# Hybrid diffusion step on one core: a pair's seven products add up in three places of the accumulator

## The chip, the cores and the metric

One Trainium2 chip, one of its cores. The kernel is one launch; what is measured is its device time in microseconds. TensorE multiplies matrices into PSUM, the accumulator. VectorE and ScalarE read PSUM and work on SBUF, GpSimd does a few fills, and SyncE issues the transfers from and to the main memory.

## The reference

Two layers with the same form run over 512 latent tokens and 128 context tokens, 640 in all, of 1024 features each. Per layer:

```python
shift1, scale1, gate1, shift2, scale2, gate2 = split(silu(cond) @ w_ada + b_ada)
h = rms_norm(x) * (1 + scale1) + shift1
q, k, v, og, gkf, gkb, sb, sc, sx, fx, mg = split(h @ w_in)
# A: bidirectional chunked gated linear attention, 4 heads; B: sb * conv3(sc * sx); C: Re(2-D DFT(fx))
x = x + gate1 * ((sigmoid(mg_A) * (A @ w_a_out) + sigmoid(mg_B) * (B @ w_b_out) + sigmoid(mg_C) * (C @ w_c_out)) @ w_o)
h = rms_norm(x) * (1 + scale2) + shift2
x = x + gate2 * ((silu(h @ w_gate) * (h @ w_up)) @ w_down)
```

A final RMSNorm follows, and the last attention states of the context tokens are returned as well. Everything is in fp32.

## The kernel before, in words

Features lie on the 128 partitions and tokens along the columns, in two halves of 320 (`TH`). A product in fp32 accuracy is three passes of TensorE: weights and activations are each split into a rounded high part (a cast, on ScalarE for the weights, L140) and the remainder (a subtraction on VectorE, L141), and high x high, high x low and low x high are added (`mm3`). A matmul has 128 x 128 weights and 320 columns.

Most products with 1024 features in are done for two blocks of 128 output columns at once, by `pair` (L245), with the seven products of Strassen and Winograd in place of eight. Each of the seven runs over four blocks of features and three passes, so it is 12 matmuls, and a pair is 84. There are 24 pairs in the mixer of each layer (names w1p_n: v, branch gates, convolution and Fourier inputs) and 19 in each feed-forward stage (wup_n), 86 in all.

The weights of a pair come in two loads and are taken in four chunks. Chunk a is [A11 A12] as loaded and serves two products, b and c are sums of the quarters (L162 to L168) and serve two each, d is A22 and serves one. The right-hand sides are the features h (B11, B21, B22 in the code) and the sums T1 to T4 of the token halves, which `token_sums` makes once per stage.

The names of the products, in the order of before: B11 with a, B21 with a, T2 with b, T3 with b, T1 with c, B22 with c, T4 with d. Their results go into four PSUM tiles pa, pb, pc, pd of two halves each (0:320 and 512:832). ScalarE copies the first (L265), and VectorE forms the two results by four additions (L269, L271, L275, L279) into an SBUF tile z.

PSUM is a pool of four such tiles of 1024 fp32 columns (L101), shared by pairs, the dense blocks (`dense`), the modulation products (`ada`) and the attention heads. Between two pairs of a mixer, after two of every three pairs, stand the matmuls of a quarter of a modulation vector, whose weights come as two raw chunks that need no split. Attention heads and the Fourier mixing are generators that a pair advances by `tick_bg`, twice.

All loads of weights are issued by SyncE in one stream with six buffers; a new load is issued when buffers are counted as freed (by the split of chunk d, by that of a full chunk, or when a raw chunk is taken). `prefetch` (L186) splits weights ahead of their use: at each `take` it goes on until two chunks are in front of the ones taken, of which d chunks are not counted. Split weights have three buffers for high and three for low parts, and one small one for d.

The order of instructions on each engine isn't the program's. A planner puts it together when the kernel is built, from the program's order as priority, the dependences between tiles and its own estimate of times; an instruction that is not ready by that estimate is passed by later ones of the same engine. The order is fixed from then on, and semaphores hold an instruction until what it needs is done.

Of the kernel before, what the change touches and what calls it, by code (L numbers as in the profile page):

```python
# [19 lines left out]
P = 128  # L20
# [3 lines left out]
T = 640  # L24
# [24 lines left out]
def ffn_order():  # L49
    """The blocks of the second residual branch: those of one chunk's products down stand between the next's up."""  # L50
    todo = []
    for ci, (c0, n) in enumerate(FF_CHUNKS):
        for i in range(n):
            yield "up", ci, c0 + i
            for _ in range(-(-len(todo) // (n - i))):
                yield todo.pop(0)
        todo = [("down", ci, j) for j in range(KB)]


def ada_after(l, phase, i):  # L60
    """The quarters of modulation vectors made after the i-th block of a phase."""
    if phase == "mix":
        seq = [(l, v, n) for v in (G1, SH2, SC2, G2) for n in range(4)]
        return seq[i // 3 * 2 + i % 3 - 1:][:1] if i % 3 else []
    seq = [(1, v, n) for v in (SC1, SH1) for n in range(4)]
    return seq[i // 2 - 2:][:1] if l == 0 and i % 2 == 0 and 4 <= i < 20 else []
# [26 lines left out]
class Builder:  # L93
# [11 lines left out]

# [1 line left out]
    def name(self, s):  # L107
# [8 lines left out]

# [1 line left out]
    def start_stream(self, plan):  # L118
# [25 lines left out]
    def _prep(self, c):  # L144
# [11 lines left out]
        if stage == "a":  # L156
            self.hl[c] = self._split(r1, 1024)
        elif stage == "b":
            sb = self.wp.tile([P, 1024], F32, tag="ws", name=self.name("sb"), bufs=2)
            sc = self.wp.tile([P, 1024], F32, tag="ws", name=self.name("sc"), bufs=2)  # L160
            self.sums[i] = sb, sc
            nc.vector.tensor_add(sc[:, 0:512], a21, a22)  # L162
            nc.vector.tensor_sub(sb[:, 0:512], sc[:, 0:512], a11)  # L163
            nc.vector.tensor_sub(sb[:, 512:1024], a11, a21)  # L164
            self.hl[c] = self._split(sb, 1024)
        elif stage == "c":
            sb, sc = self.sums.pop(i)
            nc.vector.tensor_sub(sc[:, 512:1024], a12, sb[:, 0:512])  # L168
            self.hl[c] = self._split(sc, 1024)
        else:  # L170
            self.hl[c] = self._split(a22, 512, True)
            del self.raw[i, 0], self.raw[i, 1]
            self.freed += 2
# [12 lines left out]
    def prefetch(self, ahead):  # L186
        """Splits the weights that come next, up to some chunks ahead of the last taken."""
        self._load()
        while self.prepped < len(self.chunks):
            j = self.chunks[self.prepped][0]  # L190
            if sum(1 for q in range(self.used, self.prepped + 1) if self.chunks[q][1] != "d") > ahead:
                break
# [5 lines left out]

# [1 line left out]
    def step(self, gens):  # L200
# [19 lines left out]

# [1 line left out]
    def mm3(self, o, lh, ll, rh, rl, start, stop):  # L222
        nc = self.nc
        nc.tensor.matmul(o, lh, rh, start=start, stop=False)  # L224
        nc.tensor.matmul(o, lh, rl, start=False, stop=False)  # L225
        nc.tensor.matmul(o, ll, rh, start=False, stop=stop)  # L226

# [17 lines left out]
    def pair(self, key, h, T12, T34):  # L245
        """Two blocks of 128 columns over 8 blocks of the features and both halves of the tokens by the
        seven products of Strassen and Winograd; the two results, each [P, 2, TH]."""
        nc = self.nc

        def prod(o, w, c0, ops):  # L250
            for kb in range(4):
                sl = slice(c0 + kb * P, c0 + kb * P + P)
                self.mm3(o, w[0][:, sl], w[1][:, sl], *ops[kb], kb == 0, kb == 3)

# [3 lines left out]
        nm = "_".join(map(str, key))  # L258
        w = self.take(key, "a")
        s1 = self.wp.tile([P, TH], F32, tag="s1", name=self.name("s1"), bufs=2)  # L260
        z = self.wp.tile([P, 5 * TH], F32, tag="z", name=self.name("z"), bufs=Z_BUFS)
        zv = z.rearrange("p (n t) -> p n t", t=TH)
        pa, pb, pc, pd = (self.psum(nm + x) for x in "abcd")
        prod(pa[:, 0:TH], w, 0, B11)
        nc.scalar.copy(s1, pa[:, 0:TH])  # L265
        prod(pb[:, 0:TH], w, 512, B21)
        w = self.take(key, "b")
        prod(pb[:, 512:512 + TH], w, 0, T2)
        nc.vector.tensor_add(zv[:, 0:2], pv(pb), s1[:, None, :].to_broadcast([P, 2, TH]))  # L269
        prod(pa[:, 512:512 + TH], w, 512, T3)  # L270
        nc.vector.tensor_add(zv[:, 2], pa[:, 512:512 + TH], zv[:, 1])  # L271
        self.tick_bg()
        w = self.take(key, "c")
        prod(pc[:, 0:TH], w, 0, T1)
        nc.vector.tensor_add(zv[:, 3:5], pc[:, 0:TH][:, None, :].to_broadcast([P, 2, TH]), zv[:, 1:3])  # L275
        prod(pd[:, 0:TH], w, 512, B22)
        w = self.take(key, "d")
        prod(pd[:, 512:512 + TH], w, 0, T4)
        nc.vector.tensor_add(zv[:, 3:1:-1], pv(pd), zv[:, 3:1:-1])  # L279
        self.tick_bg()  # L280
        return zv[:, 0:4:3], zv[:, 2:5:2]

    def token_sums(self, hx):
# [3 lines left out]
        for k in range(4):  # L287
            t, u = hx[k], hx[k + 4]
            p, q = self.unit(s="t12"), self.unit(s="t34")
            nc.vector.tensor_sub(p[:, A], t[:, B], t[:, A])  # L290
            nc.vector.tensor_sub(q[:, A], u[:, B], t[:, B])
            nc.vector.tensor_sub(p[:, B], u[:, B], p[:, A])
            nc.vector.tensor_sub(q[:, B], u[:, A], p[:, B])
# [9 lines left out]

# [1 line left out]
    def consts(self):  # L305
# [31 lines left out]

# [1 line left out]
    def ada_mm(self, ps, kp, raw):  # L339
# [20 lines left out]
    def ada(self, pieces):  # L360
        """Quarters of modulation vectors; what follows the products comes one piece later."""
        for l, v, n in pieces:
# [10 lines left out]

# [1 line left out]
    def table(self, name):  # L375
        """Loads a table set behind the functions of the one before."""
        self.in_order(lambda: self.tc.keep_in_program_order(self.nc.scalar.preload_act_table_set(name)))

    def act(self, *args, **kw):
        """A function that not all table sets have."""  # L380
        self.in_order(lambda: self.nc.scalar.activation(*args, **kw))  # L381
# [44 lines left out]
    def modulate(self, half, r, xs, A, sh, out, hx):  # L426
        """Yields after each feature block's part of h."""
        nc = self.nc
# [51 lines left out]
    def boundary(self, keys, rhs, xs, g, after_x, norm, head, gk=None, tail=3):  # L480
        """The blocks that end a residual branch, the norm, and the blocks that start the next phase.

        The last few of the former and all of the latter go by halves of the tokens, so that the norm of
        one half runs beside the products of the other."""
        self.table("natural_log_exp_and_others")
# [60 lines left out]
    def start(self, x, xs, A, sh, head):  # L546
        """The first norm and the first blocks, in the order in which the vectors come in."""
        nc = self.nc
# [36 lines left out]

# [1 line left out]
    def to_tokens(self, u):  # L587
        """[P channels, T] to [P tokens, 5, P channels], in PSUM."""
        pt = self.psum("tt")
        for i in range(5):  # L590
            self.nc.tensor.transpose(pt[:, i * P:i * P + P], u[:, i * P:i * P + P], self.ident)
        return pt

# [1 line left out]
    def gla_start(self, l):  # L595
# [9 lines left out]
    def gla_head(self, l, hd, gk, qd, kd, v, yos):  # L605
# [36 lines left out]
        yield  # L642
        S = self.wp.tile([P, 5 * TH], F32, tag="z", name=self.name("S"), bufs=Z_BUFS)[:, 0:NCHUNK * P]
        sv = S.rearrange("p (n e) -> p n e", e=P)
# [54 lines left out]

# [1 line left out]
    def conv(self, l, j, sc, sx):  # L701
# [11 lines left out]

# [1 line left out]
    def dft_load(self):  # L715
# [8 lines left out]
    def fourier(self, l, fxn, fr):  # L724
        """The Fourier mixing of both sequences. The even frequencies of the latent tokens come from the sums
        of the two halves of the positions, the odd ones from their differences."""
        nc = self.nc
# [86 lines left out]

# [1 line left out]
    def make_plan(self):  # L816
# [52 lines left out]

# [1 line left out]
    def gated(self, l, b, j, br, y, out):  # L871
# [202 lines left out]

# [1 line left out]
def _blocks(w):  # L1076
# [82 lines left out]
```

## Time and profile before

| | us |
|---|---|
| median of 3 runs (2074.26 to 2076.05) | 2075.63 |
| span of the profiled execution | 2075.0 |
| TensorE busy | 2012.5 |
| VectorE busy | 1570.5 |
| ScalarE busy | 919.4 |
| GpSimd busy | 18.2 |

The span is from the first to the last instruction of one profiled execution; the runs' times are of other executions. In the profile PE is TensorE, PEld its weight loads, DVE is VectorE, ACT ScalarE, SP SyncE. Matmuls overlap in the pipeline, so that each is shown for 0.31 us although one starts every 0.147 us in a dense stretch. L265 is line 265 of the kernel before.

### The profile page before, as it was taken

To read this page: it belongs to the slowest core of one execution; us is meant where nothing else is said; L and a number is where in the kernel's file an instruction comes from. 1 tells how busy PE (TensorE), PEld (TensorE's weight loads), DVE (VectorE), ACT (ScalarE), POOL (GpSimd) and SP (SyncE) were. 2 spreads that over 40 slices of the span, in tenths; PEclk is the share of its full clock that TensorE was granted. 3 is DMA by queue.
4 is the path that set the end of the run, shared out by engine and by line. 5 is a ranking of instruction groups with operands and counts; after the bars stand their busy time and mean duration, and the time that the engine had idled before them with its cause. 6 is when DMAs were issued, how large, how long until landed. Compare 5 with 4: busy or idle time off the path is not lost. (4 is left out here: it accounts for less than half of the span.)

```text
span 2075.0 us, 35216 instructions
## 1 busy us (share of the span) xinstructions
PE 2012.5 (97%) x14100; PEld 1936.3 (93%) x14100; DVE 1570.5 (76%) x2508; ACT 919.4 (44%) x1445; POOL 18.2 (1%) x52
## 2 busy tenths in 40 slices
PE   5999999999999999999999999999999999999997
PEld 2999998999999999999979999899999999999997
DVE  5778798877667777777677878898765787877876
ACT  5554435445445333333365454544543643333333
POOL 2000000000000000000000000000000000000000
PEclk9999999999999999999999999999999999999999
DMA  8254442554612333333232453335545222222222
GB/s 320 69 171 136 148 140 95 186 197 141 210 55 62 103 118 98 105 114 103 83 126 84 165 171 132 118 129 173 192 153 173 62 64 78 78 92 71 88 72 71
DMA packets 107139, 256.72 MB, mean 124 GB/s; under 512 B 13344, under 2 KB 46304, under 8 KB 106976
## 3 DMA queue, kind: packets, MB, share of 16 engines
q1 hardware_dynamic: 102528, 250.91, 36.8%
q8 instruction: 111, 1.82, 0.4%
q10 hardware_dynamic: 3728, 2.49, 0.4%
q0 software_dynamic: 720, 1.07, 0.1%
q14 instruction: 52, 0.43, 0.1%
HBM read 227.69 MB, written 26.74 MB: 123 GB/s over the span
## 5 line engine op out<-in xcount | busy, mean ns | idle before, releaser
L140 ACT CAST whi<-raw 128x1024 fp32r<-128x1024 f32 (+2 forms) x368 | 270.1, 734 | 529.5 <-PE wo L242 37.3
L141 DVE TENSOR_TENSOR wlo<-raw,whi 128x1024 fp32r<-128x1024 f32 (+2 forms) x368 | 304.4, 828 | 112.2 <-ACT whi L140 111.8
L242 PE MATMUL wd<-ffhi,whi 128*128 128x320 f32 x656 | 150.2, 310 | 0.0
L242 PE MATMUL wd<-fflo,whi 128*128 128x320 f32 x656 | 149.5, 309 | 0.0
L242 PE MATMUL wd<-ffhi,wlo 128*128 128x320 f32 x656 | 149.4, 309 | 0.0
L140 ACT CAST whi<-sb 128x1024 fp32r<-128x1024 f32 x86 | 90.3, 1050 | 125.7 <-PE wd L242 31.5
L140 ACT CAST whi<-sc 128x1024 fp32r<-128x1024 f32 x86 | 90.3, 1050 | 107.8 <-PE wd L242 48.0
L141 DVE TENSOR_TENSOR wlo<-sc,whi 128x1024 fp32r<-128x1024 f32 x86 | 104.9, 1220 | 30.2 <-ACT whi L140 29.6
L473 DVE SCALAR_TENSOR_TENSOR x<-wd,mod,x 128x512 f32<-128x512 f32 x212 | 106.7, 545 | 23.0 <-PE wd L242 23.0
L242 PEld LDWEIGHTS wd<-ffhi,whi 128*128 128x128 f32 x656 | 109.4, 188 | 3.3 <-ACT whi L140 3.3
L141 DVE TENSOR_TENSOR wlo<-sb,whi 128x1024 fp32r<-128x1024 f32 x86 | 104.8, 1219 | 6.8 <-ACT whi L140 6.7
L242 PEld LDWEIGHTS wd<-ffhi,wlo 128*128 128x128 f32 x656 | 109.7, 188 | 0.0
L242 PEld LDWEIGHTS wd<-fflo,whi 128*128 128x128 f32 x656 | 109.6, 188 | 0.0
L162 DVE TENSOR_TENSOR sc<-raw 128x512 f32<-128x512 f32 x86 | 59.3, 689 | 27.3 <-DMA raw<-in_w 26.0
L342 PE MATMUL ada<-raw,cond 128*32 128x256 f32 x768 | 56.5, 410 | 9.2 <-ACT cond L381 5.5
L163 DVE TENSOR_TENSOR sb<-sc,raw 128x512 f32<-128x512 f32 x86 | 59.1, 687 | 0.5
L168 DVE TENSOR_TENSOR sc<-raw,sb 128x512 f32<-128x512 f32 x86 | 59.1, 687 | 0.3
L242 PE MATMUL wb<-bhi,whi 128*128 128x320 f32 x256 | 59.2, 312 | 0.0
L164 DVE TENSOR_TENSOR sb<-raw,raw 128x512 f32<-128x512 f32 x86 | 59.0, 686 | 0.0
L242 PE MATMUL wb<-bhi,wlo 128*128 128x320 f32 x256 | 58.4, 309 | 0.0
L242 PE MATMUL wb<-blo,whi 128*128 128x320 f32 x256 | 58.3, 309 | 0.0
L342 PEld LDWEIGHTS ada<-raw,cond 128*32 128x32 f32 x768 | 20.8, 114 | 31.7 <-issue 7.2
(2254 smaller groups left out, 6417.0 us busy)
## 6 DMA issues: line engine op xcount, KB each, us to landing
raw<-in_w SPq DMA_DIRECT2D x104, 512.0 KB, 4.4
raw<-in_w_ada SPq DMA_DIRECT2D x96, 512.0 KB, 3.8
raw<-in_wu SPq DMA_DIRECT2D x88, 512.0 KB, 3.6
raw<-in_wd SPq DMA_DIRECT2D x96, 192.0 KB, 2.3
sgd<-z SPq DMA_DIRECT2D x48, 320.0 KB, 3.1
sgl<-sgd SPq DMA_DIRECT2D x48, 320.0 KB, 3.8
raw<-in_wb SPq DMA_DIRECT2D x48, 256.0 KB, 2.8
raw<-in_wo SPq DMA_DIRECT2D x16, 512.0 KB, 3.5
```

The source lines that it names most:

```text
L140: self.nc.scalar.copy(hi[:, 0:n], src)
L141: self.nc.vector.tensor_sub(lo[:, 0:n], src, hi[:, 0:n].bitcast(F32))
L162: nc.vector.tensor_add(sc[:, 0:512], a21, a22)
L163: nc.vector.tensor_sub(sb[:, 0:512], sc[:, 0:512], a11)
L164: nc.vector.tensor_sub(sb[:, 512:1024], a11, a21)
L168: nc.vector.tensor_sub(sc[:, 512:1024], a12, sb[:, 0:512])
L242: nc.tensor.matmul(o[h], w[:, sl], rhs[kb][h][part], start=(kb == 0 and first), stop=(kb == nk - 1 and last))
L342: self.nc.tensor.matmul(ps[32 * j:32 * j + 32, 0:256], self.cond[:, 4 * kp + j, :], r[:, j, :], start=(kp == 0), stop=(kp == 1))
L473: self.nc.vector.scalar_tensor_tensor(seg(xv), seg(v), g[:, j, i:i + 1], seg(xv), ALU.mult, ALU.add)
```

## The change

`pair` takes two PSUM tiles instead of four, and uses three places in them: r1 (first half of the first tile), r3 and r2 (the two halves of the second). The order of the products becomes B11, T2, B21, T3, T1, T4, B22. B11, T2 and T1 start r1, r2 and r3; the other four add onto what stands there, after it was read. ScalarE reads r1 twice, VectorE reads r2 twice, r3 once and at the end both halves of the second tile in one addition. Signs of the weight sums (L163, L164, L168) and of the token sums (L290 to L293) change accordingly. The tile z has 4 x 320 columns instead of 5 x 320, and s has 640 instead of 320. The first `tick_bg` now stands ahead of T3 instead of behind it.

In `prefetch` raw chunks (kind "r", the modulation weights) no longer count among the two chunks in front.

```diff
             nc.vector.tensor_add(sc[:, 0:512], a21, a22)
-            nc.vector.tensor_sub(sb[:, 0:512], sc[:, 0:512], a11)
-            nc.vector.tensor_sub(sb[:, 512:1024], a11, a21)
+            nc.vector.tensor_add(sb[:, 0:512], sc[:, 0:512], a11)
+            nc.vector.tensor_add(sb[:, 512:1024], a11, a21)
...
-            nc.vector.tensor_sub(sc[:, 512:1024], a12, sb[:, 0:512])
+            nc.vector.tensor_add(sc[:, 512:1024], a12, sb[:, 0:512])
...
-            if sum(1 for q in range(self.used, self.prepped + 1) if self.chunks[q][1] != "d") > ahead:
+            if sum(1 for q in range(self.used, self.prepped + 1) if self.chunks[q][1] not in "dr") > ahead:
...
-                self.mm3(o, w[0][:, sl], w[1][:, sl], *ops[kb], kb == 0, kb == 3)
+                self.mm3(o, w[0][:, sl], w[1][:, sl], *ops[kb], first and kb == 0, kb == 3, skip_group_check=not first)
...
-        pa, pb, pc, pd = (self.psum(nm + x) for x in "abcd")
-        prod(pa[:, 0:TH], w, 0, B11)
-        nc.scalar.copy(s1, pa[:, 0:TH])
-        prod(pb[:, 0:TH], w, 512, B21)
-        w = self.take(key, "b")
-        prod(pb[:, 512:512 + TH], w, 0, T2)
-        nc.vector.tensor_add(zv[:, 0:2], pv(pb), s1[:, None, :].to_broadcast([P, 2, TH]))
-        prod(pa[:, 512:512 + TH], w, 512, T3)
-        nc.vector.tensor_add(zv[:, 2], pa[:, 512:512 + TH], zv[:, 1])
+        u2, n1 = s[:, 0:TH], s[:, TH:2 * TH]
+        p1, p2 = self.psum(nm + "x"), self.psum(nm + "y")
+        r1, r3, r2 = p1[:, 0:TH], p2[:, 0:TH], p2[:, 512:512 + TH]
+        wa = self.take(key, "a")
+        prod(r1, wa, 0, B11, first=True)
+        nc.scalar.activation(n1, r1, AF.Copy, scale=-1.0)
+        wb = self.take(key, "b")
+        prod(r2, wb, 0, T2, first=True)
+        nc.vector.scalar_tensor_tensor(u2, n1, -1.0, r2, ALU.mult, ALU.subtract)
+        prod(r1, wa, 512, B21)
+        nc.scalar.copy(zv[:, 0], r1)
+        del wa
         self.tick_bg()
-        w = self.take(key, "c")
-        prod(pc[:, 0:TH], w, 0, T1)
-        nc.vector.tensor_add(zv[:, 3:5], pc[:, 0:TH][:, None, :].to_broadcast([P, 2, TH]), zv[:, 1:3])
-        prod(pd[:, 0:TH], w, 512, B22)
-        w = self.take(key, "d")
-        prod(pd[:, 512:512 + TH], w, 0, T4)
-        nc.vector.tensor_add(zv[:, 3:1:-1], pv(pd), zv[:, 3:1:-1])
+        prod(r2, wb, 512, T3)
+        nc.vector.tensor_add(zv[:, 3], r2, n1)
+        del wb
+        wc = self.take(key, "c")
+        prod(r3, wc, 0, T1, first=True)
+        nc.vector.tensor_sub(zv[:, 3], zv[:, 3], r3)
+        prod(r2, self.take(key, "d"), 0, T4)
+        prod(r3, wc, 512, B22)
+        nc.vector.tensor_add(zv[:, 1:3], pv(p2), s.rearrange("p (n t) -> p n t", t=TH))
         self.tick_bg()
-        return zv[:, 0:4:3], zv[:, 2:5:2]
+        return zv[:, 0:2], zv[:, 2:4]
...
-            nc.vector.tensor_sub(p[:, A], t[:, B], t[:, A])
-            nc.vector.tensor_sub(q[:, A], u[:, B], t[:, B])
-            nc.vector.tensor_sub(p[:, B], u[:, B], p[:, A])
+            nc.vector.tensor_sub(p[:, A], t[:, A], t[:, B])
+            nc.vector.tensor_sub(q[:, A], t[:, B], u[:, B])
+            nc.vector.tensor_add(p[:, B], u[:, B], p[:, A])
```

## Rows read from the trace of the kernel before

**Rows 1.** The page: span, and busy time by engine (share, instructions).
```profile
span 2075.0 us, 35216 instructions
...
PE 2012.5 (97%) x14100; PEld 1936.3 (93%) x14100; DVE 1570.5 (76%) x2508; ACT 919.4 (44%) x1445; POOL 18.2 (1%) x52
```

**Rows 2.** Windows: stretch, busy by engine, clock, DMA; mixers, then feed-forward pairs.
```profile
78.00:451.00 373.00, 365.09 (x2649) 345.93 (x2651) 305.86 (x472) 178.39 (x272) 3.66 (x13) 0.99 0.43 144
...
1097.50:1469.50 372.00, 362.27 (x2644) 342.85 (x2647) 307.27 (x474) 179.26 (x274) 3.67 (x13) 1.00 0.43 144
...
655.00:1022.00 367.00, 367.00 (x2572) 360.73 (x2571) 273.64 (x421) 130.86 (x188) 0.00 (x0) 1.00 0.31 100
...
1670.00:2029.00 359.00, 359.00 (x2451) 358.99 (x2449) 275.15 (x407) 130.46 (x183) 0.00 (x0) 1.00 0.26 79
```

**Rows 3.** Chain of waits in the feed-forward stage: start, length, what.
```profile
1686.25 7.92 PE wd L242 x54
1706.49 7.92 PE wd L242 x54
```

**Rows 4.** TensorE's waits: product, releaser, total us, times, longest.
```profile
PE w1p_17a L224 <- DVE z L279: 4.1, 2, 2.3
...
PE w1p_36a L224 <- DVE z L279: 2.9, 2, 1.5
...
PE w1p_44b L224 <- DVE z L279: 2.0, 2, 1.6
...
PE w1p_10b L224 <- ACT whi L140: 1.6, 2, 0.8
PE w1p_38a L224 <- ACT s L265: 1.1, 2, 0.6
...
PE w1p_4a L225 <- DVE tlo L302: 0.6, 1, 0.6
```

**Rows 5.** Timeline of feed-forward pair 6: start, length, engine, line, instruction [idle <- releaser].
```profile
1731.85 0.31 PE L224 MATMUL wup_6a<-hhl,whi 128*128 128x320 f32 x1
...
1733.61 0.31 PE L224 MATMUL wup_6b<-hhl,whi 128*128 128x320 f32 x1
...
1733.81 0.43 ACT L265 COPY s<-wup_6a 128x320 f32<-128x320 f32 x1 [0.95 <-PE wup_6a L226]
...
1735.47 0.51 ACT L140 CAST whi<-raw 128x384 fp32r<-128x384 f32 x1 [1.23 <-PE wup_6b L225]
1735.50 0.68 DVE L163 TENSOR_TENSOR sb<-sc,raw 128x512 f32<-128x512 f32 x1
...
1737.33 0.82 DVE L269 TENSOR_TENSOR z<-wup_6b,s 128x640 f32<-128x640 f32 x1
...
1738.89 0.31 PE L224 MATMUL wup_6c<-thi,whi 128*128 128x320 f32 x1
...
1739.09 0.49 DVE L271 TENSOR_TENSOR z<-wup_6a,z 128x320 f32<-128x320 f32 x1 [0.94 <-PE wup_6a L226]
...
1744.37 0.82 DVE L279 TENSOR_TENSOR z<-wup_6d,z 128x640 f32<-128x640 f32 x1 [0.80 <-PE wup_6d L226]
```

**Rows 6.** Timeline of mixer pair 38, second layer, around L265's copy.
```profile
1211.84 0.31 PE L224 MATMUL w1p_38c<-thi,whi 128*128 128x320 f32 x1
...
1212.24 0.42 ACT L265 COPY s<-w1p_38a 128x320 f32<-128x320 f32 x1
...
1212.72 0.41 PE L224 MATMUL w1p_38a<-thi,whi 128*128 128x320 f32 x1 [0.57 <-ACT s L265]
```

**Rows 7.** Timeline of mixer pair 18, second layer: the product behind T3, and L271.
```profile
1344.52 0.31 PE L224 MATMUL w1p_18c<-thi,whi 128*128 128x320 f32 x1
...
1350.17 0.48 DVE L271 TENSOR_TENSOR z<-w1p_18a,z 128x320 f32<-128x320 f32 x1
```

**Rows 8.** Windows of 4 us behind pair 17's wait, first layer (columns as in rows 2).
```profile
296.00:300.00 4.00, 3.49 (x14) 3.49 (x15) 3.94 (x7) 0.00 (x0) 0.00 (x0) 0.57 0.49 197
300.00:304.00 4.00, 4.00 (x29) 4.00 (x29) 4.00 (x8) 2.58 (x4) 0.00 (x0) 1.00 0.52 137
```

More of the change, by code (lines that the diff above doesn't have):

```diff
@@ L219, in drain, with mm3 @@
             self.tick()
-    def mm3(self, o, lh, ll, rh, rl, start, stop):
+    def mm3(self, o, lh, ll, rh, rl, start, stop, **kw):
         nc = self.nc
-        nc.tensor.matmul(o, lh, rh, start=start, stop=False)
-        nc.tensor.matmul(o, lh, rl, start=False, stop=False)
-        nc.tensor.matmul(o, ll, rh, start=False, stop=stop)
+        nc.tensor.matmul(o, lh, rh, start=start, stop=False, **kw)
+        nc.tensor.matmul(o, lh, rl, start=False, stop=False, **kw)
+        nc.tensor.matmul(o, ll, rh, start=False, stop=stop, **kw)
     def mm3h(self, ps, w, kb, rhs, half, start, stop):
@@ L248, in pair, with prod @@
         nc = self.nc
-        def prod(o, w, c0, ops):
+        def prod(o, w, c0, ops, first=False):
             for kb in range(4):
                 sl = slice(c0 + kb * P, c0 + kb * P + P)
-                self.mm3(o, w[0][:, sl], w[1][:, sl], *ops[kb], kb == 0, kb == 3)
+                self.mm3(o, w[0][:, sl], w[1][:, sl], *ops[kb], first and kb == 0, kb == 3, skip_group_check=not first)
         T1, T2 = [t[0] for t in T12], [t[1] for t in T12]
@@ L258, in pair @@
         nm = "_".join(map(str, key))
-        w = self.take(key, "a")
-        s1 = self.wp.tile([P, TH], F32, tag="s1", name=self.name("s1"), bufs=2)
-        z = self.wp.tile([P, 5 * TH], F32, tag="z", name=self.name("z"), bufs=Z_BUFS)
+        s = self.wp.tile([P, 2 * TH], F32, tag="s1", name=self.name("s1"), bufs=2)
+        z = self.wp.tile([P, 4 * TH], F32, tag="z", name=self.name("z"), bufs=Z_BUFS)
+        u2, n1 = s[:, 0:TH], s[:, TH:2 * TH]
         zv = z.rearrange("p (n t) -> p n t", t=TH)
-        pa, pb, pc, pd = (self.psum(nm + x) for x in "abcd")
@@ L642, in gla_head @@
         yield
-        S = self.wp.tile([P, 5 * TH], F32, tag="z", name=self.name("S"), bufs=Z_BUFS)[:, 0:NCHUNK * P]
+        S = self.wp.tile([P, 4 * TH], F32, tag="z", name=self.name("S"), bufs=Z_BUFS)[:, 0:NCHUNK * P]
         sv = S.rearrange("p (n e) -> p n e", e=P)
```

## The prediction

> **What bounds the kernel now.** I read the page's first part, then the stages one by one, then the waits. The page shows TensorE busy for 2012.5 of 2075.0 us [rows 1], so what can be won is time in which it stands still, and where that lies decides all. The windows give it by stage [rows 2]. In the pairs of the two feed-forward stages TensorE is busy for 367.00 of 367.00 us and 359.00 of 359.00 us. In the two mixer stages it is busy for 365.09 of 373.00 and 362.27 of 372.00 us, so 7.9 and 9.7 us are idle. The chain of waits says the same of the second of them: blocks down of 7.92 us begin 20.24 us apart [rows 3], and the 12.32 us between them are 84 matmuls (seven products of twelve) at 0.147 us each. A product begins 1.76 us after the one before it [rows 5], so a pair there runs without a gap. The 38 pairs of the two feed-forward stages can lose and not gain. All gain is in the 48 pairs of the mixers, and its ceiling is their 17.6 us idle, with what a halved clock adds.
>
> The waits of TensorE name the causes [rows 4]. Three groups, 4.1, 2.9 and 2.0 us, are a pair's product that waits for L279, the last addition of the pair before: a pair holds all four tiles of the accumulator, and they come back only when VectorE has read them. 1.6 us wait for a cast by ScalarE, 1.1 us for the copy at L265, 0.6 us for the token sums. A wait also slows what follows it: the granted clock is 0.57 in the 4 us behind the 2.3 us wait of pair 17 and 1.00 in the next 4, and 14 matmuls took 3.49 us where 29 then take 4.00 [rows 8]. [...]
>
> **The change, part by part.** *Evacuation.* Today a pair costs VectorE 0.82 + 0.49 + 0.82 + 0.82 = 2.95 us (L269, L271, L275 of L269's form, L279) and ScalarE one copy of 0.43 us [rows 5]. Afterwards VectorE does three operations of 320 columns and one of 640. The addition and the subtraction are L271's form, 0.49 us. The scalar_tensor_tensor of 320 from the accumulator is not in the trace; between L271's 0.49 and the 640-column 0.82, I take 0.49, for its size. Sum 0.49 x 3 + 0.82 = 2.29 us, 0.66 us less per pair, 57 us less over 86 pairs. ScalarE gets a second copy, 37 us more in all. Neither engine sets the end, so both are worth nothing by themselves. Signs in the weight and token sums turn subtractions into additions of the same size and count: nothing. Smaller z tiles and larger s tiles move no instruction.
>
> *Accumulator tiles.* A pair takes two tiles instead of four. The next pair's first product then needs one tile, and three of four are other than the one that the last addition still reads. The waits for L279 go: -9.0 us, and -1.6 us for the stretch at the lower clock behind one of them. What is late next there is the weight split; it is done one to two chunks ahead, and I count nothing for it.
>
> *The lead of the splits.* Where modulation chunks lie between two pairs, the next pair's a and b chunks are cast, summed and subtracted only as the modulation chunks are taken; afterwards during the pair before. That is per pair two casts, three sums of 0.68 us and two subtractions, moved ahead on ScalarE and VectorE, none added. SyncE's raw loads follow the count of freed buffers, which moves with chunk d and with a modulation chunk's own take, and neither take moves: no load passes another. The 1.6 us wait for the cast goes. b is needed one product sooner than today (T2 is second instead of third), and this pays for it. Bounds: 0 to -1.6; I take -1.6, since the waits named are of pair 10, behind a modulation chunk.
>
> *New waits inside the pair.* B21 goes onto r1, which ScalarE must have read; T3 onto r2 behind u2; T4 onto r2 and B22 onto r3 behind their reads. While TensorE waits, everything behind it on its queue waits too. In the feed-forward stage the readers are prompt: ScalarE's copy begins at 1733.81, 0.20 us behind the product's last slot at 1733.61, and L271 at 1739.09, 0.20 us behind 1738.89 [rows 5]. So a read is over 0.20 + 0.49 = 0.69 us behind its product, and the product in between lasts 1.76. Even behind L163, which VectorE begins at 1735.50, u2 would end at about 1735.50 + 0.68 + 0.49 = 1736.67, ahead of T3's turn at 1737.13. If that cover were gone, each such wait would cost 0.69 us.
>
> Two waits have no product between. In the trace a product that writes one half of an accumulator tile waits for a reader of the other half: pair 38's first T3 matmul, into the second half of tile a, starts at 1212.72, right behind L265's copy of the first half, which began at 1212.24 and took 0.42 us [rows 6]. r3 and r2 are halves of one tile. So T1 must wait for the addition that reads r2, and T4 for the subtraction that reads r3, 0.69 us + 0.06 us = 0.75 us each behind the product before. What covers them is other ready work, since the planner fills a gap by single matmuls: one of tile c stands ahead of tile a's in the same rows. In the feed-forward stage that is a block down, whose weights can be cast from the end of B21 on. (Today the cast waits for B21 as well, in rows 5 at 1735.47; B21 is now the third product, 1.76 us later, and the block is needed four products after.) In the mixer it is modulation products, the attention heads' matmuls and the next pair's first product. Covered, both cost 0; uncovered 0.75 us, or 1.5 us a pair. I take 0, because matmuls that are ready lie behind nearly every pair.
>
> [...]
>
> Where readers are late, slack shrinks. ScalarE's copy in pair 38 is late today and holds T3, the fourth product; afterwards it holds the third, up to 1.76 us more in each of two layers. Bounds 0 to +3.5, I take +1.0, near today's 1.1 us. T2 needs the token sums one product sooner, again 0 to +3.5 over two layers; +1.0, by today's 0.6 us.
>
> *The sum.* -9.0 - 1.6 - 1.6 + 1.0 + 1.0 = -10.2 us on a span of 2075.0: 2064.8. The median of the runs is 0.6 us above that span, so 2065.4 us.
>
> **The rivals.** *Waits inside the pair are not covered in the mixer (slower).* Place: T1 of each of 48 pairs, behind the addition that reads r2. For it: VectorE runs late there. In pair 18 T3 ends at 1344.52, L271 begins at 1350.17, 5.65 us later [rows 7]; today nobody waits for it, afterwards T1 and T4 do. Against it: VectorE has 0.66 us less per pair and the planner knows the waits. Price 0.75 us x 48 = 36 us, with the terms above 2065.4 + 36 = 2101; half covered 2083. It decides from 10.2/48 = 0.21 us of wait per pair on, where gain and loss are equal.
>
> *Uncovered in the feed-forward stage too.* Both waits in all 86 pairs are 1.5 x 86 = 129 us, 2194; half covered 2130. Against it stand the prompt readers and the blocks down.
>
> *Gain and new waits cancel.* The waits for L279 only move into the pairs, since what was late was VectorE, not the tiles: 2071.5 to 2079.8. For it: L279 itself began late in these pairs. Against it: a pair's addition was waited for only because no fourth tile was left.
>
> *The halves don't wait for each other.* Then T1 can itself stand in for a late T3, and the two terms of +1.0 go: 2063.4. Against it are rows 6.
>
> [...]
>
> **How the numbers follow.** The forecast, 0.40, with its own range 2059 to 2071; halves free, 0.07; cancelled, 0.20; uncovered in the mixer, 0.26; uncovered everywhere, 0.07. A measurement of this kernel can tell about 0.2% (4 us) from no change. Faster is the first two, 0.47; same 0.20; slower 0.33. The low end is all idle time of the mixers and the stretch at the lower clock gone, 2075.6 - 17.6 - 1.6 = 2056. The high end takes in the first rival whole, with a clock loss: 2104.
>
> **What would show it.** Right: no pair's first product waits for VectorE's last addition; TensorE busy for 359 of 359 us in the feed-forward window, with matmuls of blocks down between T3, T1 and T4; VectorE some 57 us less busy, ScalarE some 37 us more. Wrong: waits of T1, T3, T4 or B22 for ScalarE or VectorE inside pairs that add up to over 10 us, pairs in the feed-forward stage longer than 12.32 us without foreign matmuls in them, or more stretches of halved clock.

## The result: 3.4% slower

The changed kernel takes 2147.1 us (median of 4 runs), the kernel before 2075.8 us in the same rounds: a ratio of 1.0344, 95% interval 1.0329 to 1.0359. The forecast was 2065.4 us.

The page after, to be read against [rows 1]: span, and busy time by engine.

```profile
span 2141.3 us, 35262 instructions
...
PE 2057.4 (96%) x14100; PEld 1949.5 (91%) x14100; DVE 1520.8 (71%) x2508; ACT 942.7 (44%) x1531; POOL 18.2 (1%) x52
```

TensorE has the same 14100 matmuls. VectorE is 49.7 us less busy (57 were forecast) and ScalarE 23.3 us more (37 were forecast), and neither helped. By stage, the windows from the first matmul to the last of the mixers' pairs, and of feed-forward pairs 4 to 21 (the columns are those of [rows 2]):

```profile
75.60:474.80 399.20, 382.72 (x2677) 353.03 (x2676) 295.09 (x470) 184.80 (x294) 3.65 (x13) 0.99 0.41 136
1127.40:1533.60 406.20, 385.47 (x2678) 354.88 (x2677) 296.47 (x472) 187.22 (x298) 3.66 (x13) 0.98 0.41 134
697.00:1053.00 356.00, 356.00 (x2444) 343.00 (x2444) 245.52 (x397) 126.64 (x192) 0.00 (x0) 1.00 0.33 98
1756.00:2097.00 341.00, 341.00 (x2299) 336.88 (x2298) 241.82 (x377) 123.20 (x184) 0.00 (x0) 1.00 0.26 78
```

The mixers take 805.4 us where the windows of [rows 2] have 745.0: 60 us of the 66 between the spans. Only a third of that is idle time of TensorE, which rises from 17.6 to 16.5 + 20.7 = 37.2 us. In the rest it is drawn as busy: the windows hold 62 more matmuls, of other blocks, up to 9 us at 0.147 us each (an estimate), and the matmuls follow one another more slowly: busy time is 0.143 us a matmul, of all kinds (768.2 over 5355), where [rows 2] has 0.137. The feed-forward stages look untouched, busy for 356.00 of 356.00 and 341.00 of 341.00 us, but 2299 matmuls in 341.0 us are 6.74 per us, and in [rows 2] it is 2451 in 359.0, 6.83 per us. Those stages lose too, and the busy share, which the prediction had named as its sign of being right, doesn't show it, since each matmul is drawn 0.31 us long while one starts every 0.147.

TensorE's longest waits in the mixers after, for readers of the accumulator and for fin, a result of the attention heads' recurrence (total us, times, longest):

```profile
PE ab L683 <- DVE fin L670: 5.7, 2, 3.3
...
PE w1p_8y L224 <- DVE z L285: 5.2, 2, 2.6
...
PE w1p_38y L224 <- DVE s L275: 3.4, 2, 1.7
...
PE w1p_34y L224 <- DVE z L281: 2.4, 2, 1.8
...
PE w1p_16y L224 <- DVE z L281: 1.8, 1, 1.8
PE w1p_42y L224 <- DVE z L281: 1.8, 2, 0.9
```

The waits of [rows 4] for the last addition are gone, as forecast. In their place products wait inside the pair: x is the tile of r1, y that of r3 and r2, and L275, L281 and L285 are u2, the addition and the subtraction. The first row is an attention head's matmul; what stands around it is shown below.

**Where the feed-forward stage loses.** The chain of waits around two pairs (start, length, what):

```profile
1763.35 0.73 PE wd L242 x5
1765.96 0.73 PE wd L242 x5
1770.33 6.45 PE wd L242 x44
...
1790.79 3.81 PE wd L242 x26
```

The period is 1790.79 - 1770.33 = 20.46 us where [rows 3] has 20.24. (These rows are of the second layer.) Twice in a pair five matmuls of a block down stand between products: the planner did put in the cover that I counted on. The timeline of such a place, pair 7:

```profile
1821.98 0.46 PE L242 MATMUL wd<-ffhi,whi 128*128 128x320 f32 x2
...
1822.18 0.49 DVE L281 TENSOR_TENSOR z<-wup_7y,s 128x320 f32<-128x320 f32 x1 [0.67 <-PE wup_7y L226]
1822.28 0.46 PE L242 MATMUL wd<-fflo,whi 128*128 128x320 f32 x2
1822.43 0.19 PEld L242 LDWEIGHTS wd<-ffhi,wlo 128*128 128x128 f32 x1
1822.57 0.31 PE L242 MATMUL wd<-ffhi,wlo 128*128 128x320 f32 x1
...
1822.73 0.19 PEld L224 LDWEIGHTS wup_7y<-thi,whi 128*128 128x128 f32 x1
1822.73 0.42 PE L224 MATMUL wup_7y<-thi,whi 128*128 128x320 f32 x1
...
1822.98 0.32 PE L225 MATMUL wup_7y<-tlo,whi 128*128 128x320 f32 x1
...
1824.80 0.49 DVE L285 TENSOR_TENSOR z<-z,wup_7y 128x320 f32<-128x320 f32 x1 [1.61 <-PE wup_7y L226]
...
1825.34 0.41 PE L224 MATMUL wup_7y<-thi,whi 128*128 128x320 f32 x1
...
1825.59 0.31 PE L225 MATMUL wup_7y<-tlo,whi 128*128 128x320 f32 x1
```

T3's last slot ends at 1821.98, L281 reads r2 from 1822.18 to 1822.67, and T1, which goes to the other half of the tile, starts at 1822.73, 0.06 us after the read. The five matmuls fill that time to the last slot. Yet T1's second matmul comes 0.25 us after its first, not 0.147, and T4's the same (1825.34, 1825.59): 0.10 us twice per pair, nearly the whole 0.22. The rows of PEld say where this time lies: the matmul at 1822.57 has its weights loaded from 1822.43 on, during the one before it, but the load for T1's first matmul begins at 1822.73, together with the matmul. The load was held back as well, so nothing hides it.

**Where the mixers lose.** The timeline at pair 42, second layer:

```profile
1289.38 3.38 DVE L676 SCALAR_TENSOR_TENSOR S<-S,g 64x128 f32<-64x128 f32 x9
1290.44 0.42 PE L224 MATMUL w1p_44x<-hhl,whi 128*128 128x320 f32 x1
...
1292.15 0.31 PE L226 MATMUL w1p_44x<-hhl,wlo 128*128 128x320 f32 x1
1292.80 0.49 DVE L281 TENSOR_TENSOR z<-w1p_42y,s 128x320 f32<-128x320 f32 x1
...
1293.34 0.42 PE L224 MATMUL w1p_42y<-thi,whi 128*128 128x320 f32 x1 [0.88 <-DVE z L281]
```

An attention head's recurrence holds VectorE for 3.38 us. T1 of pair 42 can't start, since the addition L281 that reads the other half stands behind the recurrence. The planner pulled in all of pair 44's first product as cover, and TensorE still waits 0.88 us. Two causes meet here: T1 waits for a half that it doesn't touch, and the read is late.

The longest wait is that of the row for fin, ahead of T1 of pair 34, second layer. T3's last matmul and two rows of VectorE there:

```profile
1213.53 0.31 PE L226 MATMUL w1p_34y<-thi,wlo 128*128 128x320 f32 x1
...
1215.99 2.00 DVE L676 SCALAR_TENSOR_TENSOR S<-S,g 64x128 f32<-64x128 f32 x5 [3.77 <-DMA S<-in_st]
...
1222.07 0.49 DVE L281 TENSOR_TENSOR z<-w1p_34y,s 128x320 f32<-128x320 f32 x1
```

T3 begins its last matmul at 1213.53, and the addition L281 that T1 waits for begins at 1222.07. VectorE wasn't busy all that time: it stood idle until 1215.99, 3.77 us in all and over 2 of them after T3, since the recurrence waited for a transfer and the read stands behind the recurrence in its order.

### The profile page after: what moved, and what is told of

The parts are those of the page before. It is cut to its first block, busy times and chain, and to the rows that moved or that the text cites. A ratio compares the mean times of both kernels' runs of the same rounds, so it can differ in the third digit from the quotient of the medians.

```text
span 2141.3 us, 35262 instructions
## 1 busy us (share of the span) xinstructions
PE 2057.4 (96%) x14100; PEld 1949.5 (91%) x14100; DVE 1520.8 (71%) x2508; ACT 942.7 (44%) x1531; POOL 18.2 (1%) x52
## 4 chain that ended last, share of the span: by engine, by line
PE 85%; DVE 8%; ACT 4%; issue 2%; DMA 1%; ACTq 0%; DVEq 0%; SPq 0%
PE wd L242 14%; PE wb L242 8%; PE wo L242 3%; PE wu L242 2%; PE ada L351 2%; PE w L242 2%; DVE wlo L141 1%; DVE S L676 1%; ACT dup L932 1%; PE o L697 1%; ACT rstd L390 1%; DMA x<-in_x 1%; PE wu L225 1%; PE wu L224 1%; PE wu L226 1%
## 5 line engine op out<-in xcount | busy, mean ns | idle before, releaser
L351 PE MATMUL ada<-raw,cond 128*32 128x256 f32 x768 | 71.1, 416 | 10.4 <-ACT cond L390 5.5
L168 DVE TENSOR_TENSOR sc<-raw,sb 128x512 f32<-128x512 f32 x86 | 59.1, 687 | 0.9
L163 DVE TENSOR_TENSOR sb<-sc,raw 128x512 f32<-128x512 f32 x86 | 59.1, 687 | 0.8
L164 DVE TENSOR_TENSOR sb<-raw,raw 128x512 f32<-128x512 f32 x86 | 58.9, 685 | 0.0
```

The source lines that it names most:

```text
L163: nc.vector.tensor_add(sb[:, 0:512], sc[:, 0:512], a11)
L164: nc.vector.tensor_add(sb[:, 512:1024], a11, a21)
L168: nc.vector.tensor_add(sc[:, 512:1024], a12, sb[:, 0:512])
L351: self.nc.tensor.matmul(ps[32 * j:32 * j + 32, 0:256], self.cond[:, 4 * kp + j, :], r[:, j, :], start=(kp == 0), stop=(kp == 1))
```

## The experiments

Ratios are to the kernel before, with 95% intervals.

**r3 in another tile.** The free half of r1's tile takes r3, and r2 is alone in the other, so that T1, T4 and B22 each have a product between them and the read of their tile. The last addition, whose two operands now lie in different tiles, is cut in two; what that does by itself wasn't tried.

```diff
-        r1, r3, r2 = p1[:, 0:TH], p2[:, 0:TH], p2[:, 512:512 + TH]
+        r1, r3, r2 = p1[:, 0:TH], p1[:, 512:512 + TH], p2[:, 0:TH]
...
-        nc.vector.tensor_add(zv[:, 1:3], pv(p2), s.rearrange("p (n t) -> p n t", t=TH))
+        nc.vector.tensor_add(zv[:, 2], r2, n1)
+        nc.vector.tensor_add(zv[:, 1], r3, u2)
```

> The changed kernel with r3 moved from the tile of r2 into the free half of r1's tile; the last addition becomes two of 320 columns. Theory H (a product waits for a reader of the other half of its tile, so T1 waits for the addition that reads r2 and T4 for the subtraction that reads r3): those two waits now have a product between them and their reader, so most of the loss goes. Feed-forward pairs take 12.32 us again with no matmuls of blocks down inside, the mixers lose some 50 of their 60 us, and the time is 2065 to 2090 us. Rival V (VectorE and ScalarE are late with the reads inside a pair, wherever the places lie): feed-forward regains its 9 us, the mixers stay about as long, 2125 to 2140 us.

2099.5 us, 1.0122 (1.0107 to 1.0137), above the range of theory H and well below that of rival V. Of the 3.44%, 2.2% is gone. The windows of the same stretches:

```profile
77.10:464.50 387.40, 371.92 (x2640) 348.85 (x2638) 297.96 (x494) 186.49 (x295) 3.66 (x13) 0.98 0.42 139
1111.50:1495.10 383.60, 369.08 (x2640) 346.18 (x2638) 299.53 (x496) 187.39 (x297) 3.67 (x13) 0.99 0.42 140
689.00:1036.00 347.00, 347.00 (x2434) 340.76 (x2434) 249.31 (x414) 127.37 (x193) 0.00 (x0) 1.00 0.32 102
1719.80:2055.10 335.30, 335.30 (x2288) 335.30 (x2287) 246.74 (x393) 124.48 (x184) 0.00 (x0) 1.00 0.27 80
```

The feed-forward windows fall from 697.0 to 682.3 us together, and in the chain of waits a block down of 7.92 us is whole again (at 1732.34) and the next begins 20.24 us later (at 1752.58). The mixers fall from 805.4 to 771.0, so by the windows the shared tile cost 14.7 us there and 34.4 us here. These are upper figures: after, the four windows hold 96 matmuls more (75 and 21), work of other blocks pulled in as cover, up to 14 us at 0.147 us each (an estimate). TensorE's idle time in the mixers falls by 7.2 us only, from 37.2 to 30.0. The mixers regained less than the 50 us expected: 26 us are left, and the rival had a part in it. The same place of pair 42:

```profile
1265.33 3.39 DVE L677 SCALAR_TENSOR_TENSOR S<-S,g 64x128 f32<-64x128 f32 x9
1268.75 0.49 DVE L281 TENSOR_TENSOR z<-w1p_42y,s 128x320 f32<-128x320 f32 x1
...
1269.30 0.41 PE L224 MATMUL w1p_42y<-thi,whi 128*128 128x320 f32 x1 [2.06 <-DVE z L281]
```

Now it is T4 that waits, for the read of its own place, and T1 has gone ahead. The recurrence still stands before the read.

**The lead alone**, in the kernel before:

```diff
-            if sum(1 for q in range(self.used, self.prepped + 1) if self.chunks[q][1] != "d") > ahead:
+            if sum(1 for q in range(self.used, self.prepped + 1) if self.chunks[q][1] not in "dr") > ahead:
```

> The kernel before with the lead alone changed: raw modulation chunks are not counted. Theory H says that the loss is in the pair, so this is within 8 us of before, and the 1.6 us wait for the cast in pair 10 is gone. Rival L (the sums and casts of the next pair, now made during this one, come ahead of the reads on VectorE and ScalarE): slower than before by 10 us or more.

2079.7 us, 1.0025 (1.0015 to 1.0036), a small loss. The wait of pair 10 for the cast no longer stands among the longest, but others came (total us, times, longest):

```profile
PE w1p_46d L224 <- DVE z L269: 4.6, 2, 2.6
...
PE ada L342 <- DVE z L275: 3.6, 2, 2.0
```

**The pair alone**, raw chunks counted again (the same line, the other way round):

> The changed kernel with raw modulation chunks counted again, so the pair alone. Theory H: 2140 to 2165 us, as slow as the whole change or slower, since work that fills the gaps (the next pair's first products) has its weights later. Rival L: much of the loss is the lead, so 2090 to 2120 us.

2144.8 us, 1.0333 (1.0312 to 1.0354), not to be told from the whole change at 1.0344. The loss is the pair's.

**r3 in another tile, no lead:**

> r3 in the free half of r1's tile, and raw modulation chunks counted as before. Theory H: near the run with r3 moved and the lead (2065 to 2095 us), a few us slower if the lead helps, since nothing has to be filled with the next pair's products. Rival L: clearly faster than the run with the lead, by 10 us or more.

2102.5 us, 1.0136 (1.0120 to 1.0152), against 1.0122 with the lead; above the range of theory H, as the run with the lead was. The lead is nothing here either.

**Reads first.** With r3 in r1's tile, the five reads that a product waits for are put ahead in the planner's order:

```diff
+        with self.tc.high_priority():
+            nc.scalar.activation(n1, r1, AF.Copy, scale=-1.0)
...
+            nc.vector.scalar_tensor_tensor(u2, n1, -1.0, r2, ALU.mult, ALU.subtract)
...
+            nc.scalar.copy(zv[:, 0], r1)
...
+            nc.vector.tensor_add(zv[:, 3], r2, n1)
...
+            nc.vector.tensor_sub(zv[:, 3], zv[:, 3], r3)
```

> r3 in the free half of r1's tile, and the five reads that a later product waits for (both of ScalarE, u2, the addition and the subtraction on VectorE) put ahead of all else in the planner's order. Theory R (what is left after the halves are parted, some 25 us, is reads that stand on VectorE and ScalarE behind the attention heads' work, the state recurrence above all): most of it goes, 2070 to 2085 us, and the waits of T4 for the addition (16 us in all with r3 moved) nearly vanish. Rival Q (places that are added onto are a chain of product and read, and two tiles are too few to bridge it however prompt the reads): 2092 to 2100 us.

2076.5 us, 1.0005 (0.9995 to 1.0015): level with before. The mixers, and VectorE at pair 42:

```profile
75.50:447.10 371.60, 364.19 (x2641) 343.29 (x2639) 295.53 (x494) 186.48 (x296) 3.66 (x13) 1.00 0.43 145
1093.90:1465.70 371.80, 364.02 (x2640) 343.22 (x2638) 297.46 (x496) 187.42 (x297) 3.66 (x13) 1.00 0.43 145
```

```profile
1240.76 0.73 DVE L682 SCALAR_TENSOR_TENSOR S<-S,g 64x128 f32<-64x128 f32 x2 [0.80 <-DMA S<-in_st]
1241.41 0.47 DVE L285 TENSOR_TENSOR z<-w1p_42y,s 128x320 f32<-128x320 f32 x1
...
1242.43 0.73 DVE L682 SCALAR_TENSOR_TENSOR S<-S,g 64x128 f32<-64x128 f32 x2
1243.18 0.49 DVE L290 TENSOR_TENSOR z<-z,w1p_42x 128x320 f32<-128x320 f32 x1
1243.70 2.62 DVE L682 SCALAR_TENSOR_TENSOR S<-S,g 64x128 f32<-64x128 f32 x7
```

The two reads (L285, L290) now cut the recurrence in three, and no product of pair 42 waits. The mixers are down to 743.4 us with as many matmuls: late reads were 27.6 us. That takes in what the clock costs behind the waits, since the mixers' granted clock was 0.98 and 0.99 with r3 moved and is 1.00 here; idle time falls by 14.8 us, from 30.0 to 15.2. Rival Q falls.

**Background work later.** With r3 in r1's tile, and without the reads first:

```diff
-        self.tick_bg()
         prod(r2, wb, 512, T3)
         nc.vector.tensor_add(zv[:, 3], r2, n1)
+        self.tick_bg()
```

> r3 in the free half of r1's tile, and the first call of the background work behind the addition that reads r2, where it stood in the kernel before, instead of ahead of T3. Theory R: the recurrence that this call issues no longer comes ahead of that addition, so T4's waits shrink, 2078 to 2092 us. Rival Q: no change, 2097 to 2103 us.

2093.9 us, 1.0084 (1.0069 to 1.0099), between the two forecasts, against 1.0122 with the call where the change has it: 0.4% of the 1.2% that were left. The place of this call is a part of the lateness and not most of it.

**The change as it is, reads first** (the same five lines ahead, r3 and r2 still halves of one tile):

> The change as it is (r2 and r3 halves of one tile), with the five reads put ahead of all else. Theory: halves (some 45 us) and late reads (some 25 us) are two costs that add up, so about 2115 to 2128 us, with feed-forward pairs still some 0.2 us longer than before. Rival: it was lateness that made the halves dear in the mixer, and then the time falls to 2085 to 2105 us.

2122.3 us, 1.0218 (1.0203 to 1.0233). So the two costs add up, nearly: parting the halves takes off 2.2% and prompt reads 1.3%, and both together 3.4%. Feed-forward periods stay at 20.46 us (blocks down at 1749.71 and 1770.17), which prompt reads can't change.

**Both, and the background work later:**

> r3 moved, background call later, and reads first, all together. Theory R: as with the reads first or a few us better, 2068 to 2083 us; if it falls below 2070 it is faster than the kernel before. Rival Q: 2092 us or more.

2079.5 us, 1.0017 (1.0007 to 1.0026). With the reads first the place of the call brings nothing.

**All reads first.** As with the reads first, the two last additions too:

```diff
+        with self.tc.high_priority():
+            nc.vector.tensor_add(zv[:, 2], r2, n1)
+            nc.vector.tensor_add(zv[:, 1], r3, u2)
```

> r3 moved and all reads of the accumulator first, the two last additions too. Theory: the waits that are left in the mixer for those additions (some 4 us of modulation products, 1 us of pairs) go, and the time is 2066 to 2074 us, level with before or a little faster. Rival: the reads put first push the weight splits back and the waits turn up there, 2074 to 2082 us.

2070.7 us, 0.9982 (0.9974 to 0.9991): faster than the kernel before by 0.2%, about the least that can be told from no change, and the lowest median of all that ran.

```profile
span 2068.3 us, 35316 instructions
...
PE 2013.3 (97%) x14100; PEld 1934.2 (94%) x14100; DVE 1533.3 (74%) x2594; ACT 945.8 (46%) x1531; POOL 18.2 (1%) x52
```

**The kernel before, reads first** (L265, L269, L271, L275 and L279 put ahead in the same way):

> The kernel before with its five reads of the accumulator put first. If what cost 9 us in its mixers (first products waiting for the last addition of the pair before) is late reading and not the number of tiles, these waits go without any change to the pair: 2062 to 2070 us. If it is the tiles, or the reads first delay the splits as much, 2072 to 2080 us.

2073.0 us, 0.9994 (0.9984 to 1.0003), no difference. Of the 9.0 us of [rows 4] its trace still has 7.5 (L284 is the last addition there; total us, times, longest):

```profile
PE w1p_17a L224 <- DVE z L284: 3.2, 2, 2.1
...
PE w1p_36a L224 <- DVE z L284: 2.2, 2, 1.1
PE w1p_44b L224 <- DVE z L284: 2.1, 2, 1.2
```

Prompt reads alone don't take these waits out of the kernel before; whether it is the four tiles that keep them there wasn't tried by itself.

**All reads first, no lead:**

> As with all reads first and r3 moved, but raw modulation chunks counted again. Without the lead the next pair's splits come later and compete less with the reads, which are now first anyway: within 4 us of the run with the lead. Where the waits left are for splits, the lead shows as 3 to 8 us gained.

2072.5 us, 0.9988 (0.9980 to 0.9997), against 0.9982 with the lead: within the intervals of each other.

## Why the prediction was wrong

The sign was wrong and the time lies above the range. Two steps failed: cover was given no price, and late reads by VectorE were left out of the sum. Step by step:

- *The waits for the last addition go (-9.0 us, with the clock -10.6):* they went, but the time didn't come with them. The 1.6 us for the clock is 3.49 - 14 x 4.00/29 by [rows 8], an estimate from one stretch that no run shows by itself. With the halves parted and five reads first, nothing is left of the gain (1.0005); with all reads first it is 0.2%, some 4 us. Others of about the same length stand in their place: with the reads first, modulation products wait 3.9 us for the pair's last additions (L293), and products of pairs 46, 18 and 30 wait 3.3, 1.9 and 1.6 us for the subtraction and u2, 10.7 us together.
- *The evacuation is off the path:* right. VectorE is 49.7 us less busy, with no gain, and the scalar_tensor_tensor took 0.48 us (L275 of pair 7) where 0.49 was assumed.
- *The lead (-1.6 us):* wrong in size, within 0.3% of nothing in all four comparisons; the sign in the kernel before is a loss.
- *A write waits for the reader of the other half:* right, and it is the largest cause, 2.2 of the 3.4%. Read off one wait in [rows 6], it was shown by moving r3.
- *"Covered, both cost 0; uncovered 0.75 us, or 1.5 us a pair. I take 0, because matmuls that are ready lie behind nearly every pair":* this is the step that failed. The cover was there, and it has a price. In the feed-forward stage of the second layer it filled the gap to the last slot, and the pair still lost 0.22 us, since a product that was held back starts slowly (0.25 us to its second matmul, not 0.147). In the mixers the windows fell by 34.4 us when the halves were parted; 7.2 us of that is idle time, up to 11 us the matmuls pulled in (75 at 0.147 us, an estimate), and the rest slower matmuls. The figure is close to the 36 us of the rival "not covered in the mixer", which I gave 0.26, but by chance: that rival's price was idle time of T1. The measured 2147.1 us also lies within the span of "uncovered in the feed-forward stage too" (2130 to 2194), by chance again, since those stages were covered. And cover is used up: pair 42 had the whole first product of pair 44 in its gap and waited on.
- *Late readers (+1.0 and +1.0 us):* the second step that failed. The terms were for ScalarE's copy and for the token sums. With r3 moved, waits for ScalarE's copy (L272) are 5.6 us, above the bound of 3.5, and those for the token sums have not grown. But most of the lateness is VectorE's, which the sum had at nothing: some 22 us of waits for L275, L281 and L285. Prompt reads by both engines took 27.6 us off the mixers (771.0 to 743.4). The row that told it was in hand, L271 of pair 18 begun 5.65 us late [rows 7]; I used it for a rival and not in the sum, where 1.76 us was all the slack that a read had left.
- *The feed-forward stages can only lose:* right; they lost 14.7 us in 36 pairs by the windows with and without the shared tile, 9.0 in the first layer and 5.7 in the second. The second is 18 x 0.22 = 4.0 us and up to 1.6 us for 11 matmuls pulled in; why the first lost more isn't settled.
- *The clock:* a small share. After, the granted clock is 0.53 to 0.58 over 4 us in each of five stretches of the mixers (297:301, 379:383, 1219:1223, 1393:1397 and 1437:1441); three of the five here, the first and the third over a longer window (columns as before):

```profile
294.00:304.00 10.00, 7.60 (x47) 5.72 (x46) 6.70 (x18) 3.52 (x11) 0.00 (x0) 0.68 0.29 79
...
379.00:383.00 4.00, 4.00 (x19) 4.00 (x18) 3.54 (x5) 1.18 (x3) 0.00 (x0) 0.57 0.26 83
...
1216.00:1225.00 9.00, 6.04 (x35) 4.48 (x36) 8.39 (x20) 1.76 (x4) 0.00 (x0) 0.68 0.30 101
```

At 1.6 us each as in [rows 8], and twice that for the first and the third, which last longer, they are at most some 11 us in all (an estimate), and are part of the sums above. The third of them follows the wait of 3.3 us for fin. With the reads first, where TensorE is idle for 15.2 us and not 37.2, both mixers run at 1.00. Of the range's high end, 2104, some 3 us over the first rival's 2101 are clock, which no run shows by itself either.

The account, by the windows: mixers 34.4 us by the shared tile and 26 us more that parting it left (27.6 by late reads, less the little gained), feed-forward 14.7 us, which is 75 us; the spans differ by 66.3. The other 9 us are work of other blocks that the planner pulled into these stretches as cover and that isn't done elsewhere: after, the mixers' windows hold 62 matmuls more than [rows 2], and those of the feed-forward stage 21 more than with r3 moved, 83 in all, up to 12 us at 0.147 us each (an estimate). What isn't settled is how the rest of the 34.4 us divides into slow starts, the clock and changes between kinds of matmul.

## What to carry to other kernels

Before putting two running sums into one accumulator tile, find in a trace whether a write to one half waits for a read of the other; here one such wait told it, and the remedy was to swap halves and to cut the last addition in two. Where a product must wait for a read, the slack here is one product (1.76 us), so the reader's place in its own queue sets the time: look at the worst lag of that reader in the stage, not at its length, and put such reads first (27.6 us of the mixers here). Cover by other ready work was not free (0.22 us a pair in the second layer's feed-forward stage), so a wait that a plan "fills" should still be given a price.

## What the runs showed that I had not expected

- A matmul that starts as its semaphore comes is followed late: 0.25 us to the next instead of 0.147, though TensorE had work to the last slot before it (1822.73 and 1822.98 in pair 7). Two such places per pair are 0.2 us of 20.24. The load of its weights begins with it, at 1822.73; that of the matmul at 1822.57 begins at 1822.43, during the matmul before.
- VectorE can be late while it is idle: in pair 34 the read of a finished product stood behind work that waited 3.77 us for a transfer.
- The wait for the other half of a tile is one of the program's semaphores; that they go by tile is read from these waits (0.57 us ahead of T3 of pair 38 [rows 6], 0.88 us ahead of T1 of pair 42). The runs show the wait by tile, 2.2% of the time, and don't show what the chip would do without it; that wasn't tried.
- The same pair with the same products differs by 3.6% (ratios 1.0344 and 0.9982) by where one sum lies and in what order its reads stand.
